# Whole 16 KB ring slots for the experts in the dense part's memory, and rooms of their own for inputs and router tables

## The chip, the cores and the metric

The kernel runs on one core of a Trainium2 chip. A core has five engines with an instruction queue each: TensorE (PE, with weight loads listed as PEld), VectorE (DVE), ScalarE (ACT), GpSimd (POOL) and SyncE (SP), and 16 DMA engines, which the queues of SP, ACT and POOL feed here. On-chip memory (SBUF) has 128 partitions; a tile "128x4096" of float32 takes 16 KB in each of them, 2 MB in all. The metric is the device time of one execution in microseconds (us).

## The reference

256 tokens of 1024 features go through three blocks and a mixture of experts:

```
x = first_block(x, ...)    # twice: ffn, convolution or attention, ffn
x = second_block(x, ...)   # latent attention and block attention, gated; ffn with a convolution
h = rms_norm_3(x, norm_mix_w); proj = h @ w_in                  # third block
merged = sigmoid(gate_a) * (att @ w_branch_attn) + sigmoid(gate_s) * (ssd @ w_branch_ssd)
x = x + merged @ w_out
h2 = rms_norm_3(x, norm_ffn_w)
x = x + hierarchical_moe(h2, ...)    # 64 experts in 8 groups; 2 of the best group's 8 for each token
return rms_norm_3(x, final_norm_w)
...
def expert_block(args):
    xblk, e = args
    hid = silu(xblk @ w_gate[e]) * (xblk @ w_up[e])     # 1024 -> 512
    return hid @ w_down[e]                              # 512 -> 1024
```

All is float32. An expert's three matrices are 6.29 MB.

## The kernel before

**Dense part** (to about 1940 us). x lies as 8 chunks of 128 features by 256 tokens. Each weight matrix comes in pieces of up to 1 MB through SP's queue (L428) into three buffers `raw`; ACT rounds a piece to its high part `wh` (L444), DVE takes the rest as the low part `wl` (L445), and PE multiplies both with the high and low halves of the input. These halves are made by `split` (ACT L620 for the high, DVE L621 for the low half) out of x, or of another stage's result, and lie in units of `up`, a pool of 24 tiles of 4 KB in each partition that hands its tiles round: inputs of the stages, results between stages, attention's operands, rope tables and later the router's constants `rconst` and weights `wr` all take units `u` of it. The order on each engine is not written out: a scheduler sets it when the kernel is built, from the dependences and the pools' rooms.

**Foreseeing** (`foresee`, L1507 on). Near the end of the third block two experts are guessed from the first chunks of x, and fetched before the routing is known. Each needs three slots of 16 KB; a slot is four `up` units, and each unit has a transfer of its own of 512 KB (L1565).

**Experts** (`moe`). The routing orders the experts by their tokens; 42 have some here, and one of them a second block of tokens. The ring holds nine slots, three experts: slots 0 to 5 are the 24 `up` units that `foresee` filled, slots 6, 7 and 8 are whole tiles `ring` in pools of their own (8 lies where `xk` was and comes last). `load(j)` (L1807) reads the expert's number into a register and issues its slots on SP's queue, 4 transfers for a slot of units, 1 for a whole tile (L1816); it is called two experts ahead, and each transfer waits until the block that read the slot's former content is through. Transfers carry `cond=n1 > j`: for an expert without tokens the instruction is stepped over without moving data. So two of three experts come as 12 transfers of 512 KB, the third as 3 of 2 MB. `block` multiplies 64 tokens with gate and up (L1894, L1896), applies silu and product (L1900, L1901), and multiplies with down (L1914, L1916); the weighted result goes into the sums `po` during the next block (L1884). The order is written out by hand in this part. Beyond the last expert with tokens all engines branch out (L1936).

**End.** SP fetches the final gain `fin` into the first unit of slot 0 (L1943), ACT sums the squares of `po` (L1948), DVE multiplies `po` with the gain (L1950), and then computes the factor of the norm (L1951 and the lines of `newton2`); both scale, and the result goes out.

Of the kernel before, what the change touches and what calls it, by code (L numbers as in the profile page):

```python
# [11 lines left out]
F = mybir.dt.float32  # L12
# [13 lines left out]
# experts by place: two that are loaded ahead, then the others, the one with the most tokens at place BIG, whose next  # L26
# ones follow it; those of the 8th most and on come first. RANK: the place in the order of the numbers of tokens
BIG = 7
RANK = [0, 1] + list(range(9, 7 + BIG)) + list(range(2, 9)) + list(range(7 + BIG, NEXP))
# blocks of up to 64 tokens of an expert: the first of each expert, then what the first two and the largest of the  # L30
# others can have more, as at most 7, 3, 2 experts have over 64, 128, 192 of the 512 places
# [6 lines left out]
UNITS = 24  # L38
# [6 lines left out]
# products whose sums have PSUM banks of their own rather than half a bank  # L45
# [11 lines left out]
# steps of the last product before the router's first sums: more than the 16 of its first two chunks  # L57
# [7 lines left out]
def _lin_pieces(kc, sizes, kp):  # L65
    """(first chunk, end, first k, end) of each piece; chunks of several pieces go in pairs"""
    pieces, c = [], 0
    if kp < kc:
        for c in range(0, len(sizes), 2):
            for k in range(0, kc, kp):  # L70
                pieces += [(c, c + 1, k, k + kp), (c + 1, c + 2, k, k + kp)]
        return pieces
    for n in sizes:
        pieces.append((c, c + n, 0, kc))
        c += n
    return pieces
# [134 lines left out]
def _const(cc, cz, a, b):  # L211
    """constants a to b: those from negl to ident in cz, exact in float32r, the others in cc"""
    o, e = CC["negl"][0], CC["inv3"][0]
    return cc[:, a:b] if b <= o else cc[:, a - e + o:b - e + o] if a >= e else cz[:, a - o:b - o]
# [122 lines left out]
def weave(n, first, second, fill, per, lag=1):  # L337
    """first(i) and, lag rounds later, second(i); then per steps of fill, and what second(i) returns, if anything"""
# [11 lines left out]
def newton(nc, v, y, t):  # L350
    """y = v ** -0.5"""
# [10 lines left out]
def newton2(nc, v, y, t):  # L362
    """y = v ** -0.5 for two columns, whose steps alternate; t: [P, 4]"""
# [16 lines left out]
class Main:  # L380
# [19 lines left out]
    def chunks(self, n):  # L400
        """n chunks [P, T]"""
# [3 lines left out]
    def tokens(self):  # L405
        """two token tiles [P, D]"""
# [24 lines left out]
    def load_split(self, dram, off, blocks, width=P):  # L431
        """one piece of weights, as a function from its block number to the high and low parts"""
# [21 lines left out]
    def linear(self, name, xk, epi, c_from=0, c_to=None, wide=0, one=True, among=None):  # L454
        """a generator, one step per piece of weights (the first wide of them as one, by k);
        xk(k): [P, 2T] float32r, high halves then low halves;
        epi gets the chunks that a piece completes, [(chunk, PSUM)], the products with the low halves in columns of
        their own unless one is set; a step of among follows each k of each chunk"""
# [33 lines left out]
        def bank(c):  # L492
            """the place of chunk c: half a bank if it has one sum"""
# [74 lines left out]
    def evac(self, pss, outs, rb=None):  # L568
        """outs = the sums, times rb"""
# [6 lines left out]
    def evac2(self, pss, outs, rb):  # L576
        """outs = the sums of the halves times rb"""
# [6 lines left out]
    def resid2(self, scale):  # L584
        """x += scale times the sums of the halves"""
# [26 lines left out]
    def split(self, src, dst, scale=None):  # L612
        """dst[:, :T] = high half of src * scale, dst[:, T:] = the rest, exactly"""
# [10 lines left out]
    def split_units(self, n):  # L624
        us = [self.tl(self.up, [P, 2, 2 * T], "u", R32) for _ in range((n + 1) // 2)]
        return lambda k: us[k // 2][:, k % 2]

    def colsum(self, srcs, square=True, scale=None, per=1):
        """[P, T] in PSUM: over all features, the same in every partition"""
# [25 lines left out]
    def colsum2(self, srcs, out, scale=None, per=4, first=True):  # L655
        """out: [P, 2] in PSUM, sums of squares over all features by token; the first use of its bank or not"""
# [13 lines left out]
    def spread(self, rc, r):  # L670
        """r: two columns of tokens as a row in every partition"""
# [5 lines left out]
    def scaled(self, gname, cols=None):  # L677
        """x * g, split, and the rstd that is still to be applied, computed once the next weights are under way"""
        dst = self.split_units(8)
# [29 lines left out]
    def renormed(self, g1, g2):  # L709
        """for x = rms_norm(x) * g1, to be set by calling the last result, what scaled(g2) would give of it. With  # L710
        S = sum x^2 and S1 = sum (x g1)^2 the product of both rstds is (S1 / D + eps (S / D + eps)) ** -0.5"""
# [3 lines left out]
        dst = self.split_units(8)  # L715
# [24 lines left out]
    def normed(self, r, g):  # L740
        """x * r * g, split"""
        nc = self.nc
        dst = self.split_units(8)
# [6 lines left out]
    def row(self, a):  # L750
        """two columns of tokens as a row in every partition of PSUM"""
# [33 lines left out]
    def conv_module(self):  # L785
# [6 lines left out]
        # the shift m of the layer norm: the mean of the first seven chunks  # L792
# [27 lines left out]
        def epi(items):  # L820
# [8 lines left out]
            if j == 1:  # L829
                # not ahead of the work of the parts before  # L830
# [8 lines left out]
        # d = y - m, of which only the last chunk has a sum  # L839
# [33 lines left out]
    def stick(self):  # L873
# [18 lines left out]
        def pair(j):  # L892
            """logits of two heads and their softplus"""
# [40 lines left out]
    def rope(self, xs, tabs, half, ys):  # L934
        """ys = rotated xs; every 2 * half rows of a chunk are a head, and tabs its cosines and sines (the first half
        of those negative)"""
# [12 lines left out]
    def softmax(self, parts, scale, neg=None):  # L949
        """parts: (qT, kT) pairs contracted and summed, times scale or, by q, minus neg; returns exp(s - max)  # L950
        [P, (q0k0 | q1k0 | q1k1)] and its sums"""
# [53 lines left out]
    def second_attn(self):  # L1005
# [4 lines left out]
        xk, r, _, finish = self.renormed("fg1", "an2")  # L1010
# [30 lines left out]
        # the rstd of q goes into the softmax  # L1041
# [46 lines left out]
    def gates(self, name, xk, dst, bias, c0, r=None):  # L1088
        """tanh(z / 2), from which sigmoid(z) = (1 + tanh(z / 2)) / 2"""
# [12 lines left out]
    def gated(self, name, y, g):  # L1102
        """g = (1 + g) * (y @ w)"""
# [8 lines left out]
    def merge(self, ga, wb, yb, gb, wo, among=None):  # L1112
        nc = self.nc
        ms = self.split_units(8)
# [79 lines left out]
    def third_mix(self):  # L1194
# [29 lines left out]
        # step sizes and lam: x @ w as [high; low] of w times (high | low) of x, whose four parts are summed  # L1224
# [45 lines left out]
        # running sums of da within each half of the tokens, by head and token (twice, as high and low parts), and  # L1270
        # by token and head: nb = the sums at the token k of a block, minus them, minus them plus what is between
# [20 lines left out]
        # differential attention  # L1292
# [36 lines left out]
        # convolved inputs of the other branch  # L1329
# [69 lines left out]
        def half(i):  # L1399
            """the decays times C.B of two heads, for blocks of tokens (k, q): (1, 1), (0, 0), (0, 1)"""  # L1400
# [12 lines left out]
            for hh in range(2):  # L1413
# [5 lines left out]
                # above the diagonal, where cb is 0, any finite exponential will do  # L1419
# [65 lines left out]
    def route_consts(self):  # L1485
        nc = self.nc
        self.rcn = self.tl(self.up, [P, D], "u")
        nc.scalar.dma_start(self.rcn[:, :sum(n for _, n in RC.values())], self.ap["rconst"])
        self.wrb = self.tl(self.up, [P, D], "u")
# [7 lines left out]
    def logits(self, k):  # L1497
        """adds the part of chunk k to the router's sums"""
# [8 lines left out]
    def foresee(self):  # L1507
        """a generator: guesses from the first two chunks of x the two experts with the most tokens and loads them.
        They come first in route(), whether they have any tokens or not"""
# [41 lines left out]
        # what puts them first: more tokens than any other can have  # L1551
# [5 lines left out]
        self.ring = []  # L1557
        for j in range(2):
            e = nc.values_load(it[0:1, j:j + 1], engines=[ET.SP], min_val=0, max_val=NEXP - 1,
                               skip_runtime_bounds_check_because="the expert of a one-hot column")  # L1560
            for i in range(3):
                us = [self.tl(self.up, [P, D], "u") for _ in range(4)]
                for q, u in enumerate(us):
# [415 lines left out]
```

## Time and profile before

| what | us |
|---|---|
| median of 3 runs (lowest to highest) | 2597.13 (2595.78 to 2599.96) |
| profiled execution: span from first to last instruction | 2596.5 |
| what lies around the span | 0.6 |
| PE busy | 2477.3 (95%) |
| DVE busy | 1578.1 (61%) |
| ACT busy | 1266.9 (49%) |
| DMA queue of SP: share of 16 engines | 60.1% |
| SP's transfers of quarters, waited for by its queue | 131.8 |

The slices of the page divide the span in 40 equal parts of 65 us; a digit is the busy share in tenths. The granted clock of PE is 0.985 of full speed over the span. Window rows give, for each stretch, the busy time and the count of instructions of each engine, then the granted clock, the mean busy share of the DMA engines (a little over 1 when they are full), and the rate in GB/s. Timeline rows give start, duration, engine (a q behind it for its queue: branches, DMA issues), line, operation, output and input tile, count, and in brackets the idle time before it with what ended it. A row with "x24" stands for 24 instructions from the first's start to the last's end.

### The profile page before, as it was taken

What the parts mean: (1) busy time and instruction counts of PE and PEld (TensorE: products, weight loads), DVE (VectorE), ACT (ScalarE), POOL (GpSimd) and SP (SyncE); (2) the same over time, 40 slices, a digit from 0 to 9 for tenths busy, and PEclk for the clock granted to TensorE, in tenths of its full rate; (3) what the DMA queues carried; (4) which work ended last, traced back from release to release, by engine and by line L of the source; (5) the groups of instructions that cost most, each with busy time, mean ns of one, the idle gap of its engine ahead of it and who ended that gap; (6) DMA issues with size and microseconds to landing.
All of it is one profiled execution on the core that took longest, in us unless ns stands there. A gap on an engine that the chain in (4) does not pass through costs nothing. (4 is left out here: it accounts for less than half of the span.)

```text
span 2596.5 us, 41179 instructions
## 1 busy us (share of the span) xinstructions
PE 2477.3 (95%) x15468; PEld 1919.1 (74%) x15468; DVE 1578.1 (61%) x3128; ACT 1266.9 (49%) x2402; POOL 29.1 (1%) x62
## 2 busy tenths in 40 slices
PE   8999999999999999999999999999978989999885
PEld 7889888888888888989999889988972333333221
DVE  7768887687654876876799688987751111111111
ACT  6546665565555555765566587966531101111101
POOL 0000000000000000000000000000000000000000
PEclk9999899999999999999999999999989999999998
DMA  6554055555542556434554654434478999999995
GB/s 236 178 190 146 33 179 179 179 196 178 200 156 98 179 174 207 168 131 152 182 184 163 200 181 145 165 115 140 168 288 341 398 378 414 412 417 413 418 413 228
DMA packets 103901, 579.18 MB, mean 223 GB/s; under 512 B 12033, under 2 KB 13057, under 8 KB 68353
## 3 DMA queue, kind: packets, MB, share of 16 engines
q1 hardware_dynamic: 101520, 573.49, 60.1%
q8 instruction: 132, 2.16, 0.3%
q10 hardware_dynamic: 2016, 2.13, 0.3%
q14 instruction: 89, 0.72, 0.1%
q0 software_dynamic: 144, 0.67, 0.1%
HBM read 587.78 MB, written 1.05 MB: 227 GB/s over the span
## 5 line engine op out<-in xcount | busy, mean ns | idle before, releaser
L444 ACT ACTIVATE wh<-raw 128x1024 fp32r<-128x1024 f32 (+1 forms) x636 | 628.1, 991 | 542.1 <-PE pl L489 258.7
L445 DVE TENSOR_TENSOR wl<-raw,wh 128x1024 fp32r<-128x1024 f32 (+1 forms) x636 | 720.8, 1136 | 219.0 <-ACT wh L444 216.2
L489 PE MATMUL pl<-u,wh 128*128 128x512 f32 x2288 | 809.6, 396 | 9.5 <-ACT wh L444 9.5
L490 PE MATMUL pl<-u,wl 128*128 128x256 f32 x2288 | 646.0, 282 | 0.0
L485 PE MATMUL pl<-u,wh 128*128 128x256 f32 x2180 | 616.0, 283 | 3.0 <-ACT u L617 1.9
L487 PE MATMUL pl<-u,wl 128*128 128x256 f32 x2180 | 612.3, 281 | 3.7 <-DVE wl L445 3.7
L486 PE MATMUL pl<-u,wh 128*128 128x256 f32 x2180 | 613.5, 282 | 0.3
L489 PEld LDWEIGHTS pl<-u,wh 128*128 128x128 f32 x2288 | 431.3, 188 | 113.2 <-ACT wh L444 10.0
L490 PEld LDWEIGHTS pl<-u,wl 128*128 128x128 f32 x2288 | 430.5, 188 | 0.3
L485 PEld LDWEIGHTS pl<-u,wh 128*128 128x128 f32 x2180 | 410.9, 189 | 7.0 <-ACT u L617 2.2
L487 PEld LDWEIGHTS pl<-u,wl 128*128 128x128 f32 x2180 | 410.6, 188 | 6.8 <-DVE wl L445 4.6
L486 PEld LDWEIGHTS pl<-u,wh 128*128 128x128 f32 x2180 | 411.4, 189 | 2.9 <-DVE u L621 0.9
L1901 DVE TENSOR_TENSOR h<-s,pgu 64x512 f32<-64x512 f32 x43 | 29.7, 692 | 491.1 <-ACT s L1900 491.1
L1894 PE MATMUL pgu<-u,xe 128*64 128x512 f32 x464 | 211.0, 603 | 18.6 <-PEq L1926 6.7
L1896 PE MATMUL pgu<-u,xe 128*64 128x512 f32 x464 | 211.1, 603 | 0.0
L1894 PEld LDWEIGHTS pgu<-u,xe 128*64 128x64 f32 x464 | 62.4, 139 | 156.5 <-issue 130.9
L1900 ACT ACTIVATE s<-pgu 64x512 f32<-64x512 f32 x43 | 25.3, 589 | 308.8 <-PE pgu L1896 308.8
L581 DVE TENSOR_TENSOR t<-pl,t 128x256 f32<-128x256 f32 x176 | 73.6, 420 | 85.9 <-ACT t L580 85.9
L1894 PE MATMUL pgu<-ring,xe 128*64 128x512 f32 x224 | 104.1, 617 | 20.2 <-DMA ring<-wexp 16.1
L1918 ACT COPY yy<-py 128x512 f32<-128x512 f32 x43 | 25.2, 585 | 177.8 <-PE py L1916 140.9
L1884 PE MATMUL po<-yy,cw 64*128 64x512 f32 x344 | 106.6, 635 | 3.3 <-ACTq L1936 3.3
L1914 PE MATMUL py<-u,hT 128*64 128x512 f32 x232 | 105.8, 598 | 0.5 <-ACT hT L1912 0.5
(450 smaller groups left out, 2852.0 us busy)
## 6 DMA issues: line engine op xcount, KB each, us to landing
u<-wexp SPq DMA_DIRECT2D x360, 512.0 KB
raw<-w_ffi SPq DMA_DIRECT2D x88, 1024.0 KB
ring<-wexp SPq DMA_DIRECT2D x42, 2048.0 KB
raw<-w_ffo SPq DMA_DIRECT2D x64, 704.0 KB
raw<-w_up SPq DMA_DIRECT2D x22, 1024.0 KB
raw<-w_in3x SPq DMA_DIRECT2D x16, 1024.0 KB
raw<-w_pw SPq DMA_DIRECT2D x12, 1024.0 KB
raw<-w_v SPq DMA_DIRECT2D x12, 1024.0 KB
```

The source lines that it names most:

```text
L444: nc.scalar.activation(wh[:, :n], src, AF.Copy)
L445: nc.vector.tensor_tensor(out=wl[:, :n], in0=src, in1=wh[:, :n].bitcast(F), op=OP.subtract)
L485: nc.tensor.matmul(ps[c], lhsT=wh, rhs=x[:, :T], start=st, stop=False, skip_group_check=True)
L486: nc.tensor.matmul(ps[c], lhsT=wh, rhs=x[:, T:2 * T], start=False, stop=False, skip_group_check=True)
L487: nc.tensor.matmul(ps[c], lhsT=wl, rhs=x[:, :T], start=False, stop=k == kc - 1, skip_group_check=True)
L489: nc.tensor.matmul(ps[c], lhsT=wh, rhs=x, start=k == 0, stop=False)
L490: nc.tensor.matmul(ps[c][:, :T], lhsT=wl, rhs=x[:, :T], start=False, stop=k == kc - 1)
L581: self.each(lambda o, t, p: nc.vector.tensor_tensor(out=o, in0=p[:, :T], in1=t, op=OP.add), outs, ts, pss)
L1884: nc.tensor.matmul(po[t_ * 2 + dh], lhsT=cw[64 * dh:64 * dh + 64, t_ * P:(t_ + 1) * P], rhs=yy[64 * dh:64 * dh + 64, :], start=False, stop ...
L1894: nc.tensor.matmul(pgu[0:64], lhsT=xj[:, k], rhs=w(k * D), start=k == 0, stop=k == 7)
L1896: nc.tensor.matmul(pgu[64:128], lhsT=xj[:, k], rhs=w(k * D + 512), start=k == 0, stop=k == 7)
L1914: nc.tensor.matmul(py[0:64], lhsT=hT[:, k], rhs=w(8 * D + k * D), start=k == 0, stop=k == 3)
```

## The change

The pool `up` has 20 units for 24. Four tiles of the same size in a pool `mx` hold the inputs of the stages that are made by `scaled`, `renormed` (for the second attention) and `normed`, and the merged branches in `merge`. The router's constants and weights get a tile `rcw` that exists from the start. In `foresee` the pool `up` is closed, and a pool `rg` is opened in its place with five whole slots: three for the first guessed expert and two for the second. Its third slot, `ring5`, lies in a pool `own` that `moe` opens, and `load(1, (2,))` fetches it there. All nine slots are whole tiles with one transfer of 2 MB each, and the tiles of the end (`fr`, `junk`, `y`) are quarters of slot 0. The room that generated DMA descriptors take on the chip is set to 8192. The rest of the diff takes out comments and docstrings.

```
-UNITS = 24
+UNITS = 20
...
-    def split_units(self, n):
-        us = [self.tl(self.up, [P, 2, 2 * T], "u", R32) for _ in range((n + 1) // 2)]
+    def split_units(self, n, own=False):
+        us = [self.tl(self.mx if own else self.up, [P, 2, 2 * T], "u", R32) for _ in range((n + 1) // 2)]
...
     def scaled(self, gname, cols=None):
-        dst = self.split_units(8)
+        dst = self.split_units(8, True)
...
     def merge(self, ga, wb, yb, gb, wo, among=None):
-        ms = self.split_units(8)
+        ms = self.split_units(8, True)
...
     def route_consts(self):
         nc = self.nc
-        self.rcn = self.tl(self.up, [P, D], "u")
-        nc.scalar.dma_start(self.rcn[:, :sum(n for _, n in RC.values())], self.ap["rconst"])
-        self.wrb = self.tl(self.up, [P, D], "u")
+        n = sum(n for _, n in RC.values())
+        self.rcn, self.wrb = self.rcw[:, :n], self.rcw[:, n:n + 648]
+        nc.scalar.dma_start(self.rcn, self.ap["rconst"])
...
         self.ring = []
+        self.upx.close()
+        rg = self.top.enter_context(self.tc.tile_pool(name="rg", bufs=1, side="right"))
         for j in range(2):
...
-            for i in range(3):
-                us = [self.tl(self.up, [P, D], "u") for _ in range(4)]
-                for q, u in enumerate(us):
-                    o = i * 4096 + q * D
-                    nc.sync.dma_start(u, self.ap["wexp"][ds(e, 1), :, o:o + D].rearrange("o p l -> p (o l)"))
-                self.ring.append(us)
+            for i in range(3 - j):
+                slot = rg.tile([P, 4096], F, name=f"ring{3 * j + i}")
+                nc.sync.dma_start(slot, self.ap["wexp"][ds(e, 1), :, i * 4096:i * 4096 + 4096].rearrange("o p l -> p (o l)"))
+                self.ring.append(slot)
...
         rts = top.enter_context(tc.tile_pool(name="rt", bufs=1))
-        up = top.enter_context(tc.tile_pool(name="up", bufs=UNITS, side="right"))
+        rcw = rts.tile([P, sum(n for _, n in RC.values()) + 648], F, name="rcw")
+        upx = ExitStack()
+        up = upx.enter_context(tc.tile_pool(name="up", bufs=UNITS, side="right"))
         with ExitStack() as ctx:
             m = Main(tc, ap, ctx)
+            m.mx = ctx.enter_context(tc.tile_pool(name="mx", bufs=4))
...
+        big = [ctx.enter_context(tc.tile_pool(name="own", bufs=1)).tile([P, 4096], F, name="ring5")]
...
-        def load(j):
+        def load(j, only=range(3)):
...
-            for i in range(3):
-                slot = ring[(3 * j + i) % NSLOT]
-                w = D if slot[0][0] is not slot[1][0] else 4096
-                for o in range(0, 4096, w):
-                    nc.sync.dma_start(slot[o // D][0][:, :w],
-                                      wx[ds(e, 1), :, i * 4096 + o:i * 4096 + o + w].rearrange("o p l -> p (o l)"),
-                                      cond=n1 > j)
+            for i in only:
+                nc.sync.dma_start(ring[(3 * j + i) % NSLOT],
+                                  wx[ds(e, 1), :, i * 4096:i * 4096 + 4096].rearrange("o p l -> p (o l)"),
+                                  cond=n1 > j)
...
         more = (n2, n3, n4)
+        load(1, (2,))
...
-        fr, junk, *y = (u for u, _ in ring[0])
+        fr, junk, *y = (ring[0][:, q * D:q * D + D] for q in range(4))
...
-    nc = _bacc.Bacc("TRN2", target_bir_lowering=False, num_devices=1)
+    nc = _bacc.Bacc("TRN2", target_bir_lowering=False, num_devices=1, dynamic_dma_scratch_size=8192)
```

The order changes in three places. First DVE's queue at the program's start, before and then after (`rcw` holds the router's constants, `cn` is a small tile of the routing, `u` are the halves of x, `wl` and `raw` the first weights):

```order
L1975 UNCONDITIONAL_BRANCH
L621 SCALAR_TENSOR_TENSOR u_90<-x,pc,u_90 128x256 x2
L621 SCALAR_TENSOR_TENSOR u_91<-x,pc,u_91 128x256 x2
L445 TENSOR_TENSOR wl_123<-raw_76,wh_122 128x1024
L445 TENSOR_TENSOR wl_127<-raw_76,wh_126 128x1024
```

```order
L1978 UNCONDITIONAL_BRANCH
L1638 COPY cn<-rcw 64x1
L621 SCALAR_TENSOR_TENSOR u_94<-x,pc,u_94 128x256 x2
L621 SCALAR_TENSOR_TENSOR u_95<-x,pc,u_95 128x256 x2
L445 TENSOR_TENSOR wl_127<-raw_80,wh_126 128x1024
L445 TENSOR_TENSOR wl_131<-raw_80,wh_130 128x1024
```

The copy out of the router's constants has moved from the routing to the head of DVE's queue; the transfer that it reads, `rcw<-rconst`, is the fifth entry of ACT's queue now, behind four small ones.

Then ACT's queue at the end of `out2`, the second block's output product, and the start of `up2` behind it (`u<-x,pc` are the high halves of `up2`'s input, `t<-x` squares of x), before and after:

```order
L444 ACTIVATE wh_13607<-raw_13605 128x1024
L620 ACTIVATE u_13566<-x,pc 128x256
L662 ACTIVATE t_13627<-x 128x256
L444 ACTIVATE wh_13611<-raw_13605 128x1024
L620 ACTIVATE u_13566<-x,pc 128x256
L662 ACTIVATE t_13630<-x 128x256
L444 ACTIVATE wh_13729<-raw_13727 128x1024
L620 ACTIVATE u_13567<-x,pc 128x256
```

```order
L444 ACTIVATE wh_13615<-raw_13609 128x1024
L663 ACTIVATE t_13634<-x 128x256
L444 ACTIVATE wh_13733<-raw_13731 128x1024
L620 ACTIVATE u_13568<-x,pc 128x256 x2
L620 ACTIVATE u_13569<-x,pc 128x256 x2
L620 ACTIVATE u_13570<-x,pc 128x256 x2
L620 ACTIVATE u_13571<-x,pc 128x256
```

The splits stood one behind each weights' split; now they stand together behind the last but one.

Last SP's queue at the end of the program, where the loads of experts 42 and 43 and the branches stand ahead of the final gain, before (its last six of 24 loads) and after (all six):

```order
L1816 DMA u_21028<-wexp 128x1024
L1816 ISA
L1816 DMA u_21029<-wexp 128x1024
L1816 ISA
L1816 DMA u_21030<-wexp 128x1024
L1936 COMPARE_AND_BRANCH x2
L1936 UNCONDITIONAL_BRANCH x51
L1943 DMA u_21011<-fin 128x1024
```

```order
L1820 DMA ring_21017<-wexp 128x4096
L1820 ISA
L1820 DMA ring_21019<-wexp 128x4096
L1820 ISA
L1820 DMA ring_21021<-wexp 128x4096
L1939 COMPARE_AND_BRANCH x2
L1939 UNCONDITIONAL_BRANCH x51
L1946 DMA ring_21017<-fin 128x1024
```

A slot's four instructions have become one, here as in every load of slots 0 to 5.

## Rows read from the trace of the kernel before

**Rows 1.** The page: PE and the DMA rate in 40 slices of the span.

```profile
PE   8999999999999999999999999999978989999885
...
GB/s 236 178 190 146 33 179 179 179 196 178 200 156 98 179 174 207 168 131 152 182 184 163 200 181 145 165 115 140 168 288 341 398 378 414 412 417 413 418 413 228
```

**Rows 2.** Windows of the expert part: busy us (instructions), clock, DMA share, GB/s.

```profile
1990.00:2010.00 20.00, 19.19 (x92) 6.16 (x90) 4.17 (x8) 2.50 (x5) 1.23 (x2) 1.00 1.01 408
...
2070.00:2090.00 20.00, 16.35 (x70) 5.73 (x68) 2.09 (x4) 1.54 (x3) 0.61 (x1) 0.91 0.86 312
...
2450.00:2550.00 100.00, 88.09 (x389) 26.45 (x385) 13.23 (x26) 9.87 (x19) 4.31 (x7) 0.98 1.02 415
```

**Rows 3.** Windows in which whole slots (three rows), then quarters, flow alone.

```profile
2144.00:2150.00 6.00, 5.17 (x26) 1.96 (x24) 0.00 (x0) 0.58 (x1) 0.00 (x0) 1.00 1.01 419
...
2280.00:2286.00 6.00, 6.00 (x32) 1.87 (x26) 0.00 (x0) 0.27 (x1) 0.00 (x0) 1.00 1.02 434
...
2371.00:2377.00 6.00, 4.42 (x22) 1.55 (x20) 0.00 (x0) 0.58 (x1) 0.00 (x0) 1.00 1.00 426
...
2207.00:2225.00 18.00, 17.19 (x84) 5.55 (x82) 4.17 (x8) 2.32 (x5) 1.09 (x2) 1.00 1.03 408
2252.00:2270.00 18.00, 17.59 (x86) 5.78 (x84) 2.08 (x4) 2.13 (x4) 0.61 (x1) 1.00 1.03 411
```

**Rows 4.** Timeline of SP's queue from 2146 us: first issue's start, time to the last.

```profile
2146.55 29.81 SPq L1816 DMA_DIRECT2D u<-wexp  x24
...
2502.15 40.61 SPq L1816 DMA_DIRECT2D u<-wexp  x24
...
2547.53 28.30 SPq L1816 DMA_DIRECT2D u<-wexp  x24
2581.80 0.36 SPq L1943 DMA_DIRECT2D u<-fin  x1
```

**Rows 5.** Timelines of PE, then ACT, then DVE from 2558 us to the end.

```profile
2558.28 1.09 PE L1894 MATMUL pgu<-ring,xe 128*64 128x512 f32 x1 [3.32 <-DMA ring<-wexp]
...
2572.75 0.59 PE L1916 MATMUL py<-ring,hT 128*64 128x512 f32 x1
...
2579.14 0.60 ACT L1948 ACTIVATE u<-po 128x512 f32<-128x512 f32 x1 [5.10 <-SPq L1936]
...
2581.79 0.19 ACT L1948 ACTIVATION_READ_ACCUMULATOR u<-po 128x1 f32 x1
...
2585.62 2.48 DVE L1950 TENSOR_TENSOR u<-po,u 128x512 f32<-128x512 f32 x4 [14.88 <-DMA u<-fin]
2588.02 0.15 DVE L1951 TENSOR_TENSOR fv<-sq 128x2 f32<-128x2 f32 x1
```

**Rows 6.** Timelines of ACT's queue, DVE and PE at the start; a window there.

```profile
2.15 0.95 ACTq L1197 DMA_DIRECT2D al<-rows  x1
...
6.87 1.68 DVE L621 SCALAR_TENSOR_TENSOR u<-x,pc,u 128x256 fp32r<-128x256 f32 x4 [6.87 <-ACT u L620]
9.32 2.36 DVE L445 TENSOR_TENSOR wl<-raw,wh 128x1024 fp32r<-128x1024 f32 x2 [0.77 <-ACT wh L444]
...
9.34 0.79 PE L489 MATMUL pl<-u,wh 128*128 128x512 f32 x1 [9.34 <-ACT wh L444]
...
12.00:14.00 2.00, 2.00 (x7) 1.70 (x7) 2.00 (x7) 2.00 (x8) 0.00 (x0) 1.00 1.00 417
```

**Rows 7.** The page's transfer of `cz` (KB, us to landing); `rconst` near the dense part's end.

```profile
cz<-consts POOLq DMA_DIRECT2D x1, 656.0 KB, 8.6
...
1810.66 0.33 ACTq L1488 DMA_DIRECT2D u<-rconst  x1
...
1815.19 0.14 DVE L1636 COPY cn<-u 64x1 f32<-64x1 f32 x1
```

**Rows 8.** ACT's timeline at the end of `out2`, and a window there.

```profile
1299.32 0.49 ACT L620 ACTIVATE u<-x,pc 128x256 fp32r<-128x256 f32 x1
...
1270.00:1310.00 40.00, 39.95 (x335) 39.32 (x334) 32.44 (x71) 23.55 (x38) 0.00 (x0) 1.00 0.53 180
```

More of the change, by code (lines that the diff above doesn't have):

```diff
@@ L707, in unhook2, with renormed @@
             hook()
-    def renormed(self, g1, g2):
+    def renormed(self, g1, g2, own=False):
         nc = self.nc
@@ L714, in renormed @@
         nc.vector.tensor_tensor(out=g, in0=self.col(g1, 0, 8), in1=self.col(g2, 0, 8), op=OP.mult)
-        dst = self.split_units(8)
+        dst = self.split_units(8, own)
         for k in range(8):
@@ L742, in normed @@
         nc = self.nc
-        dst = self.split_units(8)
+        dst = self.split_units(8, True)
         for k in range(8):
@@ L1009, in second_attn @@
             nc.scalar.dma_start(rt[a], self.ap["rope2"][:, a * T:(a + 1) * T])
-        xk, r, _, finish = self.renormed("fg1", "an2")
+        xk, r, _, finish = self.renormed("fg1", "an2", True)
         rc = self.rc
@@ L1726, in build @@
         rts = top.enter_context(tc.tile_pool(name="rt", bufs=1))
-        up = top.enter_context(tc.tile_pool(name="up", bufs=UNITS, side="right"))
+        rcw = rts.tile([P, sum(n for _, n in RC.values()) + 648], F, name="rcw")
+        upx = ExitStack()
+        up = upx.enter_context(tc.tile_pool(name="up", bufs=UNITS, side="right"))
         with ExitStack() as ctx:
             m = Main(tc, ap, ctx)
+            m.mx = ctx.enter_context(tc.tile_pool(name="mx", bufs=4))
+            m.rcw = rcw
             m.x, m.cc, m.cz = x, cc, cz
@@ L1744, in build @@
             tc.keep_in_program_order(nc.gpsimd.dma_start(cz.bitcast(R32), ap["consts"][:, o:e]))
-            m.up = up
+            m.up, m.upx, m.top = up, upx, top
             m.sp = ctx.enter_context(tc.tile_pool(name="sp", bufs=2))
@@ L1793, in moe @@
         first = ctx.enter_context(tc.tile_pool(name="first", bufs=1))
-        big = [first.tile([P, 4096], F, name=f"ring{j}") for j in range(6, NSLOT - 1)]
+        big += [first.tile([P, 4096], F, name=f"ring{j}") for j in range(6, NSLOT - 1)]
         sb = ctx.enter_context(tc.tile_pool(name="moe", bufs=1))
@@ L1801, in cst @@
             return _const(cc, cz, o + a, o + (n if b is None else b))
-        ring = [[(u, 0) for u in us] for us in ring] + [[(b, q * D) for q in range(4)] for b in big]
+        ring = ring + big
         wx = ap["wexp"]
-        def load(j):
+        def load(j, only=range(3)):
             if j >= NEXP:
@@ L1860, in moe @@
         last = ctx.enter_context(tc.tile_pool(name="last", bufs=1))
-        big = last.tile([P, 4096], F, name=f"ring{NSLOT - 1}")
-        ring.append([(big, q * D) for q in range(4)])
+        ring.append(last.tile([P, 4096], F, name=f"ring{NSLOT - 1}"))
         def window(b, dst):
@@ L1889, in w @@
             def w(o):
-                u, a = ring[(3 * j + o // 4096) % NSLOT][o % 4096 // D]
-                return u[:, a + o % D:a + o % D + 512]
+                return ring[(3 * j + o // 4096) % NSLOT][:, o % 4096:o % 4096 + 512]
             for k in range(8):
```

## The prediction

> **What bounds the kernel now.** I read the page first (engine shares and the 40 slices), then windows of the expert stage, SP's issue queue, and the timelines of the first 13 and the last 40 us. The page shows two programs one after the other [rows 1]: up to about 1940 us PE is busy in nearly every slice while the DMA engines move about 180 GB/s; behind it the slices stand at 412 to 418 GB/s. The reader is to see that PE sets the end of the dense part, and the transfers that of the expert part. The windows say it more sharply [rows 2]: from 2450 to 2550 PE is busy 88% and the DMA share is 1.02. In 2070 to 2090 that share is only 0.86: there the ring was full, PE was the later one, and the transfers waited for it. So nothing that transfers gain or lose before about 2110 reaches the end; what they do behind it does, through the last block, whose first matmul waited 3.32 us for its slot [rows 5].
>
> **The stream.** In SP's queue [rows 4] groups of three whole slots (2 MB each) alternate with 24 quarters (0.5 MB each). The group of 24 at 2146.55 is the first behind the full ring, that at 2502.15 the last with data (the 24 at 2547.53 are for experts with no tokens and move nothing). Between and with these two lie nine groups, 9 x 24 = 216 quarters, 113.2 MB. The change turns them into 54 whole slots. What that is worth is read off the stretches in which one kind flows alone [rows 3]. Six stretches of whole slots gave 419, 425, 433, 434, 423 and 426 GB/s, mean 426.7; five of quarters 409, 408, 411, 409 and 409, mean 409.2. So 113.2 MB takes 265.4 us for 276.7: **-11.3 us**. With the slowest whole and the fastest quarter stretch (419, 411) it is -5.3, with 434 and 408 it is -16.6. PE doesn't take the bound back: an expert of 6.29 MB takes 14.7 us at 426.7 GB/s. PE's last block runs from 2558.28 to 2573.3, 15.0 us, in which its first four pairs of matmuls ran 1.09 us each for 0.59 [rows 5], about 1.7 us in all; without that a block takes some 13.3 us, less than a transfer either way.
>
> The Trainium skill (DMA: Bandwidth & Descriptors, Where 436 GB/s comes from) says that for transfers between HBM and SBUF the HBM side binds at about 358 GB/s; by that the size of a transfer would change nothing here. The trace disagrees on the figure: both kinds run above 400. That the memory, and not the transfer's shape, sets the rate is nevertheless a rival below.
>
> **The tail.** The last down matmul ends at 2573.3, and the end comes 23 us later. SP is still stepping through the 24 skipped quarters (from 2547.53 for 28.30 us), takes 6.0 us of branches, and only then issues the final gain at 2581.80 [rows 4]. DVE has waited 14.88 us for it when it starts at 2585.62, and the chain L1951 starts at 2588.02 [rows 5]. With the change 6 skipped slots stand in place of 24 quarters; they wait only for the block before the last, so SP is through some 2 us behind the last block's start, and even with its 6.0 us of branches ready before 2573.3. The gain, 3.8 us from issue to its use, is then there by about 2577.5. What is late next are ACT's squares: their last read-out starts at 2581.79 and takes 0.19, so L1951 starts at about 2582.0 for 2588.02: **-6.0 us**. ACT's own delay, 5.10 us in front of the first square, is put down to SP's branch in that row; ACT passes the same branches itself, so I leave it where it is. If SP did hold it, up to 2 us more go; if the issue still comes late, nothing: 0 to -8.
>
> **The start.** `rconst` (128 rows of 1009 floats, 516 KB) moves from the dense part's end to the fifth place on ACT's queue at the very start, and the copy `cn<-rcw` that reads it becomes DVE's first instruction, ahead of the first splits of x. Queued behind that wait are all splits L621, all low halves of weights L445, and PE, whose products need both. Before, DVE began at 6.87 [rows 6], with 0.77 us idle in front of its first L445. ACT's fourth issue starts at 2.15 and takes 0.95, so rconst is issued at about 3.1. No row has this transfer beside the first loads. Bounds: on a quiet core it was issued at 1810.66 and its copy ran at 1815.19, under 4.5 us [rows 7], which would land it at 7.6 and cost nothing over the 0.77. The constants `cz`, 656 KB beside weight loads on another queue, took 8.6 us; counted from 3.1 that gives 11.7, counted from about 8, when x and the first weights are through, 16 and more, a cost of 8. I take 8.6 from the issue, since that row is the nearest in size, place and company: landing 11.7, copy 0.14, first split at 11.85, so 4.98 later, less the 0.77: **+4.2 us** (0 to +8). From 12 on PE and DVE are both busy all of the time [rows 6], so the loss isn't caught up.
>
> By the Trainium skill (DMA: Bandwidth & Descriptors, Queues, rings and completion order) an engine takes turns between the queues that it has work for, packet by packet; by that rconst would get about half of the rate and land within its lower bound. The constants' row disagrees: 656 KB in 8.6 us is 76 GB/s, a fifth of the stream. It is the first rival.
>
> **The dense part.** The split inputs get four units of their own, so each stage's input waits for the last reader of the one before. Of all stages that shows in one place: at the end of `out2` ACT's splits of x for `up2` now stand in a bunch behind the last weights' split, where before one stood between each two. Before, the last split ran at 1299.32, and PE was busy 39.95 of 40 us there [rows 8]. Eight splits at 0.49 are 3.9 us on ACT, of which PE needs the first only; the others lie beside its products, two chunks by k. I take **+0.5** (0 to +3). Fewer `up` units (20 for 24) wait for nothing else: on the other engines the order and the waits read the same. The reopening itself is hidden: expert 0 and two thirds of expert 1 are fetched into five slots from about 1900 on, the sixth a little later, and block 0 starts at 1953, after routing. I count it at nothing; if it were late, the full ring at 2070 would absorb it.
>
> **The sum** against the execution that the profile shows: 4.2 + 0.5 - 11.3 - 6.0 = -12.6. Its span was 2596.5, with 0.6 us around it, which is the median of the runs, 2597.1. So the span comes to 2583.9 and the time to **2584.5 us**.
>
> **Rivals.**
> - *The start is hidden* (rconst lands by 7.6): +0.5 - 11.3 - 6.0 = -16.8, 2580.3. For it the quiet transfer's 4.5 us; against it the constants' 8.6, and DMA engines that are full at that time, so that 516 KB has to displace something. 0.15.
> - *Whole slots are no faster as a stream*: the 6 us stretches are short, and what they gained may be given back where the kinds change over; with the memory as the bound all whole is as fast as the mixture. Then 4.2 + 0.5 - 6.0 = -1.3, 2595.8. Against it: all six stretches lie above all five others. 0.13.
> - *The tail stays* (the gain is issued late all the same, or the squares move with it): 4.2 + 0.5 - 11.3 = -6.6, 2590.5. For it: the profile blames a branch of SP for ACT's wait; against: the skipped issues fill SP up to the branches. 0.13.
> - *Slower: large transfers run below the mixture.* A slot can be refilled only when all of it is read, and counts as landed only when its slowest part is in; with fewer, larger pieces in the queue the engines may fall dry between them. The stage has shown such a rate: 408 GB/s in 1990 to 2010, at a DMA share of 1.01 [rows 2]. From 2110 to 2558 at 414 GB/s 185.5 MB move; at 400 GB/s they take 463.7 us for 448, +15.7, in all +14.4, 2611.5. It decides from 408 GB/s down, where it costs 6.5 and the total passes +5.2. Against it the same six stretches. 0.06.
> - The forecast keeps 0.53.
>
> **Numbers.** A difference of 0.2%, 5.2 us, is what a measurement can tell here. Beyond it on the fast side lie nearly all of the forecast, the first rival and a bit more than half of the third: 0.75. Within it the second rival, the rest of the third and a little of the forecast: 0.17. Beyond it on the slow side the fourth and the worst ends of the start together with the second: 0.08. All ends added give 2574 and 2602; the range with 8 in 10 is 2575 to 2597, from near the best case over the third and second rival.
>
> **What will show it.** DVE's first split at about 11.9 and PE's first product 3 to 5 us behind 9.34: the start. Windows of 100 us behind 2150 at 425 GB/s or more, and last block's first matmul some 7 us earlier than 2558.28 (4.7 later by start and boundary, 11.3 earlier by the stream): the stream. The final gain issued by the time of the last down matmul, and L1951 8.8 us behind it for 14.7: the tail. Windows at 414 would overthrow the stream's term, a first split before 8 the start's, and L1951 still waiting for the gain the tail's.

## The result, and the profile after

The changed kernel took 2577.06 us in the median of 4 runs (2575.2 to 2581.64), the kernel before 2597.86 beside it: a ratio of 0.9919, 95% interval 0.9906 to 0.9932. Run again in five rounds it took 2579.97 (2578.24 to 2582.1), ratio 0.9927 (0.9913 to 0.994). It is faster by 19 to 21 us, where 12.6 were forecast. The time lies inside the range, on its fast side.

The profiled execution of the changed kernel has a span of 2579.9 us and took 2581.64; the later profiles show 1.7 to 2.0 us around their spans, so the first profile of the kernel before stands for about 2598.2, not 2596.5 + 0.6 as the sum took it. The stream of the changed kernel, as windows (columns as in [rows 2]):

```profile
2150.00:2250.00 100.00, 96.35 (x450) 32.03 (x446) 14.60 (x28) 10.83 (x21) 4.32 (x7) 1.00 1.01 427
2250.00:2350.00 100.00, 96.76 (x454) 31.67 (x454) 16.68 (x32) 11.99 (x24) 4.94 (x8) 1.00 1.01 427
2350.00:2450.00 100.00, 94.09 (x436) 30.32 (x432) 14.59 (x28) 11.23 (x22) 4.32 (x7) 1.00 1.01 427
2450.00:2550.00 100.00, 89.31 (x410) 28.72 (x412) 14.59 (x28) 10.84 (x21) 4.32 (x7) 1.00 1.01 427
```

427 GB/s stands where [rows 2] have 415, in each window. To time the stream, take ACT's silu of block 11, the first behind the full ring, and of the last block: first the kernel before, then the changed one (timelines of ACT).

```profile
2123.95 0.59 ACT L1900 ACTIVATE s<-pgu 64x512 f32<-64x512 f32 x1 [7.40 <-PE pgu L1896]
...
2567.02 0.59 ACT L1900 ACTIVATE s<-pgu 64x512 f32<-64x512 f32 x1 [11.38 <-PE pgu L1896]
```

```profile
2127.64 0.59 ACT L1903 ACTIVATE s<-pgu 64x512 f32<-64x512 f32 x1 [7.32 <-PE pgu L1899]
...
2557.65 0.59 ACT L1903 ACTIVATE s<-pgu 64x512 f32<-64x512 f32 x1 [7.77 <-PE pgu L1899]
```

443.1 us before, 430.0 now: the stream gives 13.1. Up to 1.6 of that is PE's clock: in the kernel before PE waits 3.32 us for the last block's first slot [rows 5], and from 2558.0 to 2561.5 its granted clock is 0.51, so that four pairs of matmuls take 3.3 us, not 1.7. The changed kernel's last block starts 9.3 us sooner, without that wait and at full clock (timeline of PE):

```profile
2549.03 0.59 PE L1897 MATMUL pgu<-ring,xe 128*64 128x512 f32 x1
```

The tail, in the order of [rows 5] (timelines of PE, ACT, DVE, and SP's queue):

```profile
2563.39 0.59 PE L1919 MATMUL py<-ring,hT 128*64 128x512 f32 x1
2566.84 2.78 PE L1888 MATMUL po<-yy,cw 64*128 64x512 f32 x8 [2.86 <-ACTq L1939]
...
2568.26 0.60 ACT L1951 ACTIVATE ring<-po 128x512 f32<-128x512 f32 x1 [3.59 <-PE po L1888]
...
2568.98 2.85 DVE L1953 TENSOR_TENSOR ring<-po,ring 128x512 f32<-128x512 f32 x4 [7.61 <-ACT ring L1951]
2571.75 0.15 DVE L1954 TENSOR_TENSOR fv<-sq 128x2 f32<-128x2 f32 x1
...
2564.32 0.36 SPq L1946 DMA_DIRECT2D ring<-fin  x1
```

The final gain is issued 0.3 us behind the last down matmul (which ends at 2564.0), no longer 8.5. DVE's chain L1954 starts 7.8 us behind that matmul, before 14.7: 6.9 won. ACT's first square waits for PE now, 4.3 us behind the last down matmul; in [rows 5] it waited for SP, 5.8 behind. What the chain comes behind is DVE's own product with the gain (L1953); ACT's last square is done 0.7 us before it. The start, as in [rows 6]:

```profile
3.00 0.73 ACTq L1490 DMA_DIRECT2D rcw<-rconst  x1
...
13.08 0.14 DVE L1638 COPY cn<-rcw 64x1 f32<-64x1 f32 x1 [13.08 <-DMA rcw<-rconst]
13.21 1.67 DVE L621 SCALAR_TENSOR_TENSOR u<-x,pc,u 128x256 fp32r<-128x256 f32 x4
...
13.84 1.19 PE L489 MATMUL pl<-u,wh 128*128 128x512 f32 x2 [13.84 <-DVE u L621]
```

DVE starts 6.3 us later and PE's first product comes 4.5 later; matched matmul for matmul, PE runs 4.8 us behind the kernel before from 60 to 300 us. The trace's DMA packets show what the landing at 13.1 is made of. The 128 packets of `rconst` (4036 bytes each) run from 8.3 to 12.6 us, though it was issued at 3.0: until then ACT's queue moves packets of 512 and 256 bytes for the small transfers ahead. So it waited 5.3 us and moved for 4.3; on the quiet core, before, it moved for 2.4. That the small transfers caused the wait is read from this order; no run puts `rconst` ahead of them. So far 4.8 - 13.1 - 6.9 = -15.2. The rest is in the dense part, which the forecast had at +0.5: block 0 starts at 1952.7 for 1953.2, so the 4.8 lost at the start are won back on the way. A stretch of the first block's attention shows how. A round of two heads ends with a group of ten small products; the kernel before, then the changed one (timelines of PE):

```profile
785.51 1.54 PE L890 MATMUL pa<-a,cz 128*128 128x128 f32 x10
...
796.40 1.54 PE L890 MATMUL pa<-a,cz 128*128 128x128 f32 x10
```

```profile
781.38 1.54 PE L891 MATMUL pa<-a,cz 128*128 128x128 f32 x10
...
792.08 1.54 PE L891 MATMUL pa<-a,cz 128*128 128x128 f32 x10
```

10.89 us before, 10.70 now. PE waits for nothing in either, at a granted clock of 1.00; the linear products between (L485 to L487) follow each other at 0.113 to 0.114 us for 0.117 to 0.118.

### The profile page after: what moved, and what is told of

It reads as the page before. It is cut to its first block, busy times and chain, and to the rows that moved or that the text cites. A ratio compares the mean times of both kernels' runs of the same rounds, so it can differ in the third digit from the quotient of the medians.

```text
span 2579.9 us, 40094 instructions
## 1 busy us (share of the span) xinstructions
PE 2470.7 (96%) x15468; PEld 1910.6 (74%) x15468; DVE 1578.1 (61%) x3128; ACT 1267.1 (49%) x2402; POOL 29.2 (1%) x62
## 5 line engine op out<-in xcount | busy, mean ns | idle before, releaser
L485 PE MATMUL pl<-u,wh 128*128 128x256 f32 x2180 | 614.7, 283 | 3.3 <-ACT u L617 1.9
L487 PE MATMUL pl<-u,wl 128*128 128x256 f32 x2180 | 611.0, 281 | 4.1 <-DVE wl L445 4.1
L487 PEld LDWEIGHTS pl<-u,wl 128*128 128x128 f32 x2180 | 412.6, 189 | 7.4 <-DVE wl L445 5.1
L485 PEld LDWEIGHTS pl<-u,wh 128*128 128x128 f32 x2180 | 410.4, 189 | 7.4 <-ACT u L617 2.2
L1897 PE MATMUL pgu<-ring,xe 128*64 128x512 f32 x688 | 312.2, 605 | 29.9 <-DMA ring<-wexp 18.4
L1899 PE MATMUL pgu<-ring,xe 128*64 128x512 f32 x688 | 312.5, 605 | 0.0
L1897 PEld LDWEIGHTS pgu<-ring,xe 128*64 128x64 f32 x688 | 93.5, 139 | 233.7 <-issue 211.5
L1917 PE MATMUL py<-ring,hT 128*64 128x512 f32 x344 | 159.5, 607 | 0.5 <-ACT hT L1915 0.5
L1919 PE MATMUL py<-ring,hT 128*64 128x512 f32 x344 | 159.5, 607 | 0.0
L1917 PEld LDWEIGHTS py<-ring,hT 128*64 128x64 f32 x344 | 44.2, 138 | 108.2 <-issue 75.7
```

The lines of the kernel that those rows point to most:

```text
L485: nc.tensor.matmul(ps[c], lhsT=wh, rhs=x[:, :T], start=st, stop=False, skip_group_check=True)
L487: nc.tensor.matmul(ps[c], lhsT=wl, rhs=x[:, :T], start=False, stop=k == kc - 1, skip_group_check=True)
L1897: nc.tensor.matmul(pgu[0:64], lhsT=xj[:, k], rhs=w(k * D), start=k == 0, stop=k == 7)
L1899: nc.tensor.matmul(pgu[64:128], lhsT=xj[:, k], rhs=w(k * D + 512), start=k == 0, stop=k == 7)
L1917: nc.tensor.matmul(py[0:64], lhsT=hT[:, k], rhs=w(8 * D + k * D), start=k == 0, stop=k == 3)
L1919: nc.tensor.matmul(py[64:128], lhsT=hT[:, k], rhs=w(8 * D + k * D + 512), start=k == 0, stop=k == 3)
```

## The experiments

**The changed kernel again** (no edit).

> The changed kernel once more, for a second profile and an interval. My account: the start costs 4.9 us (DVE's first split at 13.2, PE's first product at 13.8), the stream runs at 427 GB/s from 2120 on, the final gain is on chip before the squares are done; the median stays at 2577, and the 5 us by which the profiled execution was slower than the three others is scatter of PE's clock in the dense part and in the first blocks. Rival: the profiled execution is the typical one, then the median comes to 2581.

Median 2579.97; the profiled execution had a span of 2576.5. So the rival is nearer on the median, but the executions scatter by 4 us around it. In this second profile the start, the stream (silu to silu 430.2) and the tail (7.5 us) are nearly as in the first; what differs most is PE's pace in `up2` (below). Between these two profiles the three terms agree within 0.3 us; the total doesn't.

**The copy late.** The router's transfer stays at the start, its copy goes behind the one ahead of it in the routing:

```
-        V.tensor_copy(cn[:, 0:1], pc[0:64, 0:1])
+        first = V.tensor_copy(cn[:, 0:1], pc[0:64, 0:1])
...
-        V.tensor_copy(cn[:, 3:4], rk("pmod", p=64))
+        with self.tc.issue_after(first.ins):
+            V.tensor_copy(cn[:, 3:4], rk("pmod", p=64))
```

> Only the copy out of the router's constants is put back behind the copy before it in the routing; the transfer stays at the program's start. Theory (DVE's wait for that transfer delays all by 4.9 us and nothing catches up): first split at 6.9, first product at 9.3, end 4.9 us sooner, about 2572 for 2577. Rival A (the early transfer itself takes its 1.3 us of full DMA engines from x and the first weights): 1 to 2 us less gain, 2573.5. Rival B (the dense part absorbs the late start somewhere): no gain, 2577.

2571.9 us (2571.61 to 2572.36), ratio 0.9894 (0.9879 to 0.9909). Timelines of DVE and PE:

```profile
6.96 1.68 DVE L621 SCALAR_TENSOR_TENSOR u<-x,pc,u 128x256 fp32r<-128x256 f32 x4 [6.96 <-ACT u L620]
...
9.13 0.79 PE L489 MATMUL pl<-u,wh 128*128 128x512 f32 x1 [9.13 <-ACT wh L444]
```

One instruction moved, and PE runs level with the kernel before (0.1 us ahead at 100 us). The theory's 4.9 is shown by the profile; the medians differ by 8.1, and the start doesn't explain the other 3. Rivals A and B fall: the transfer itself costs nothing at the start, and the dense part doesn't absorb the wait. This version beats both kernels, by 26.8 us against the one before.

**The transfers late too.** As far back as the scan's last square:

```
+            self.late = nc.scalar.activation(sq, xx, AF.Square)
...
+        with self.tc.issue_after(self.late.ins):
+            nc.scalar.dma_start(self.rcn, self.ap["rconst"])
...
```

> The router's three transfers are put behind the last square of the scan on ACT's queue, near where they stood before the change; the copy follows them. Theory: as with the copy alone, 2572, and at most 1.3 us better than it, since 516 KB at about 400 GB/s no longer stand among the first loads. Rival: the late transfers and copy stand in the way of the routing, as they did before, and cost 1 us or more against the copy alone.

2577.27 (2571.12 to 2580.65). Its profile (span 2569.4) has the same start as the copy alone and an end 0.8 us sooner; the runs scatter by 9.5 us. The median is 5.4 us above the copy alone's, as the rival has it, but the ratios' intervals overlap (0.9901 to 0.9929 and 0.9879 to 0.9909). Nothing is shown between the two, and the copy alone was the steadier one.

**The skipped quarters back, alone.**

```
+                w = D if j >= 42 and slot < 6 else 4096
+                for o in range(0, 4096, w):
```

> The loads for experts from 42 on, which are all stepped over, go to slots 0 to 5 in quarters again: 24 skipped issues at the end for 6, nothing else moves. Theory (the skipped issues held the final gain, and that the end): last matmul unchanged, final gain issued some 8 us behind it, end 7 us later, 2584. Rival (the tail is short for another reason, such as ACT's branches or the whole tile at the end): unchanged, 2577.

2588.39 (2587.38 to 2589.67), 8.4 more than the changed kernel beside it. Timelines of PE, ACT and DVE, and SP's queue:

```profile
2561.86 0.59 PE L1922 MATMUL py<-ring,hT 128*64 128x512 f32 x1
...
2569.30 0.60 ACT L1954 ACTIVATE ring<-po 128x512 f32<-128x512 f32 x1 [6.16 <-SPq L1942]
...
2575.99 2.48 DVE L1956 TENSOR_TENSOR ring<-po,ring 128x512 f32<-128x512 f32 x4 [16.13 <-DMA ring<-fin]
2578.39 0.15 DVE L1957 TENSOR_TENSOR fv<-sq 128x2 f32<-128x2 f32 x1
...
2571.94 0.35 SPq L1949 DMA_DIRECT2D ring<-fin  x1
```

The gain comes 9.5 us behind the last matmul, DVE waits 16.13 us for it, and the chain starts 15.9 behind that matmul, where the kernel before had 14.7 and the changed one 7.8. The skipped issues are shown to be the cause of the long tail, and ACT's first square is back to waiting for SP. In SP's queue they follow each other at 0.46 us, which for 18 more of them is 8.3 us.

**What sets the stream's rate.** Three kernels change only how slots 0 to 5 are filled for experts 2 to 41 (and in the third, where the matmuls find each quarter): four transfers of a quarter (1), two of a half (3), and two of a half whose 8 KB in a partition go to two places (4):

```
1:  w = D if 1 < j < 42 and slot < 6 else 4096
3:  w = 2 * D if 1 < j < 42 and slot < 6 else 4096
4:  dst = ring[slot].rearrange("p (a b l) -> p b a l", a=2, b=2)
    for b in range(2):
        nc.sync.dma_start(dst[:, b], src[:, :, b * 2 * D:(b + 1) * 2 * D]...)
```

> The changed kernel with slots 0 to 5 filled by four transfers of 512 KB (4 KB in each partition) again, for experts 2 to 41; the tiles stay whole, foreseen and skipped loads too. Theory (the transfer's shape sets the stream's rate): 409 GB/s where quarters flow, 414 over 100 us, last block 11 to 13 us later, 2589 for 2577. Rival (the stream gained because slots come free or are asked for sooner, not by shape): windows stay at 427, 2577.

> Slots 0 to 5 by two transfers of 1 MB, 8 KB in each partition. Theory of a fixed cost for each piece in a partition: with 409.2 GB/s for 4 KB and 426.7 for 16 KB the time per byte falls as 1/length, which gives 420.7 for 8 KB alone and a third of the loss, some 4 us, 2581. Rival (a threshold between 4 and 8 KB, or the number in flight): 427 GB/s and 2577.

> Two transfers of 1 MB for each of slots 0 to 5, as in the run with halves, but each puts its 8 KB of a partition down as two pieces of 4 KB that don't lie next to each other (the order of the quarters in the slot is changed, and the matmuls read them so). Theory (the length of the piece sets the rate): as with quarters, 414 GB/s over 100 us, about 442 us from block 11 to block 42, some 2592. Rival (the number and size of the transfers): as with halves, 422 GB/s, 432 us, 2585.

One window of each, in this order:

```profile
2250.00:2350.00 100.00, 97.17 (x454) 31.74 (x452) 14.59 (x28) 11.42 (x22) 4.30 (x7) 1.00 1.02 414
```

```profile
2250.00:2350.00 100.00, 97.17 (x453) 31.79 (x454) 15.50 (x30) 11.42 (x22) 4.30 (x7) 1.00 1.01 422
```

```profile
2250.00:2350.00 100.00, 97.17 (x454) 31.51 (x450) 14.78 (x29) 11.43 (x22) 4.92 (x8) 1.00 1.02 414
```

| filled by | transfers a slot | piece | GB/s | silu to silu, us | median, us |
|---|---|---|---|---|---|
| whole slots | 1 | 16 KB | 427 | 430.0, 430.2 | 2577.06, 2579.97 |
| halves | 2 | 8 KB | 422 | 433.7 | 2585.36 |
| halves in two pieces | 2 | 4 KB | 414 | 442.6 | 2591.28 |
| quarters | 4 | 4 KB | 414 | 444.5 | 2592.66 |

The rate goes with the length of the piece that lies together in a partition, not with the number or size of the transfers: the last two rows differ by a factor of two in number and agree in rate, the two rows of halves agree in number and differ by 8 GB/s. (Of the 1.9 us between the last two rows, up to 1.5 is again the half clock in the last block, which the run with quarters has and the one with two pieces hasn't.) Halves lose 3.6 us of the 14.4 that quarters lose, a bit less than the third that a fixed cost for each piece gives.

The traces' DMA packets show that cost itself. A packet is one piece of one partition. From 2150 to 2450 us one of 4 KB takes its engine 163 ns in the mean (164 in the run with two pieces), one of 8 KB 315, one of 16 KB 618. Four small ones so take 34 ns more than one of 16 KB, two halves 12 more: some 11 to 12 ns for each packet, whatever its length.

The Trainium skill (DMA: Bandwidth & Descriptors, Why small descriptors are slow) names such a cost, some 3 cycles for each packet, where 32 bytes take one; at 4 KB against 16 KB that is an estimate of under 2%, while the stretches of one kind in [rows 3] differ by 4%, so the direction agrees and the size doesn't.

**Quarters by partitions.** The same number of transfers with 16 KB pieces, each to 32 of the 128 partitions:

```
+                n = 32 if 1 < j < 42 and slot < 6 else P
+                for o in range(0, P, n):
+                    nc.sync.dma_start(ring[slot][o:o + n], wx[ds(e, 1), o:o + n, ...])
```

> The same four transfers of 512 KB for each of slots 0 to 5, but each of 32 partitions with the whole 16 KB of a partition. Theory (the length of the piece in a partition decides): 427 GB/s, 2577 as with whole slots. Rival (the number of transfers, their fixed cost and SP's waits for earlier ones decide): 414 GB/s, 2589, as the quarters.

3015.13 us, ratio 1.1574 (1.1547 to 1.1601): neither theory. Two windows:

```profile
2150.00:2250.00 100.00, 74.49 (x298) 24.49 (x294) 10.43 (x20) 7.74 (x15) 3.07 (x5) 0.90 1.01 281
...
2350.00:2450.00 100.00, 61.67 (x216) 19.86 (x216) 6.60 (x13) 5.24 (x10) 2.46 (x4) 0.81 1.01 231
```

The engines count as busy (1.01) at 281 and 231 GB/s; a packet of 16 KB takes 1049 ns here in the mean, for 618. A transfer to a quarter of the partitions is slow for a reason of its own, which no run here separates, so this run says nothing on the length of the piece; the run with two pieces took its place.

**PE's pace in the dense part.** Two more profiles of the kernel before came first.

> The kernel before, for a second profile. Of the five profiles with whole tiles all show the second block's up2 (1305 to 1425 us) passed 2 to 6 us sooner against the first profile of the kernel before, with PE busy throughout. Theory (PE's pace in a stage differs between executions of one program): this profile shows a gain of that kind against the first one too, or a loss elsewhere. Rival (the change made the stage shorter): the second profile agrees with the first there within 0.5 us.

> As the run before it, a third profile of the kernel before: with two more of them it is to be seen whether the pace in up2 scatters or is the same each time.

2595.07 and 2605.5 us. In both a round of heads takes 10.89 or 10.90, and `up2` passes within 0.1 us of the first profile: in three profiles the kernel before has one pace. The rival is favoured: the change made these stages shorter. Then all inputs were put back into `up`, with everything else as changed:

```
-UNITS = 20
+UNITS = 24
...
-        us = [self.tl(self.mx if own else self.up, [P, 2, 2 * T], "u", R32) ...]
+        us = [self.tl(self.up, [P, 2, 2 * T], "u", R32) ...]
```

> The changed kernel without the inputs' own room: UNITS 24 again and all split inputs in up; ring slots, router table and tail as changed. In the seven profiles of whole tiles the dense part passes 707 to 811, 1020 to 1310 and 1740 to 1850 us of the first profile's time in 5.0 us less than in the three profiles of the kernel before, each stretch alike in all of them, and up2 (1310 to 1430) in 4.3 less in most. Theory (where the inputs lie, or when they are free, sets PE's pace there): these stretches take as long as in the kernel before, block 0 starts 5 to 9 us later, 2585 to 2588. Rival (the pace hangs on the shift of PE against the other engines by the later start, or on the rest of the memory's layout): the stretches are as short as in the changed kernel, 2579.

2585.74 (2580.27 to 2594.59), 6 us slower than the changed kernel run on its own. Half of that is the start: the router's constants land at 15.0 us in this profile, and PE runs 8.0 us behind the kernel before, not 4.8. Timeline of PE:

```profile
783.57 1.54 PE L891 MATMUL pa<-a,cz 128*128 128x128 f32 x10
...
794.47 1.54 PE L891 MATMUL pa<-a,cz 128*128 128x128 f32 x10
```

10.90 us again, and of 5.0 us that the stretches named in the expectation had gained 3.6 are lost. The exception is `up2`: it keeps its quicker pace here, as in seven of the nine profiles with the changed layout, so that part (4.3 us in those executions, nothing in the other two, of which the first profile is one) isn't due to the inputs' room. Nor is the later start the cause: with the copy late PE is level with the kernel before, and the same stretches are 5.0 us shorter. Last, the inputs keep their room, but it lies behind the weight buffers, which move by 16 KB with it, as does the small tile `pc`; no engine's order changes:

```
-            m.mx = ctx.enter_context(tc.tile_pool(name="mx", bufs=4))
...
             m.wp = ctx.enter_context(tc.tile_pool(name="wp", bufs=4))
+            m.mx = ctx.enter_context(tc.tile_pool(name="mx", bufs=4))
```

> The changed kernel with the inputs' own room behind the weight buffers on chip instead of ahead of them; the order of every engine is the same. In the first block's attention a round of two heads takes 10.70 us on PE in the changed kernel and 10.90 in the kernel before and with inputs in up. Theory (their room being their own, that is when it is free and what else shares it, sets the pace): 10.70, and 2579 in all. Rival (the place on chip sets the pace): another pace, 10.90 or between, and the time of the dense part moves with it.

2585.29 (2584.26 to 2590.01). Timeline of PE:

```profile
779.04 1.54 PE L891 MATMUL pa<-a,cz 128*128 128x128 f32 x10
790.03 1.54 PE L891 MATMUL pa<-a,cz 128*128 128x128 f32 x10
```

10.99 us: slower than either, with the same instructions in the same order. Other stages are quicker for it: from 811 to 1020 us of the first profile's time this run gains 3.1 us on the kernel before, the changed kernel 0.1. So it isn't that the inputs have a room of their own, nor when it is free, but where inputs and weight buffers lie on the chip. Which of them, and by what mechanism, stays open.

## Why the prediction was right, and what it had missed

- **The stream** was right in mechanism and rate: 426.7 GB/s forecast, 427 measured, -11.3 forecast, -13.1 measured. The size was off by the count: the group of 24 quarters at 2102.70 us, issued as the ring filled, was left out of the 216; with its 12.6 MB the same rates give -12.6. Beside the rate, the measured 13.1 holds up to 1.6 of half clock in the last block, which the sum left out. The rival of no gain had a condition, the memory as the bound, that the runs with quarters and with two pieces refute; a rate below the mixture's, as the slower rival has it, appears only with transfers to 32 partitions, which the change doesn't make.
- **The tail** was right: -6.0 forecast, -6.9 measured. The step left open, whether SP holds ACT's squares, came out on the fast side (1.5 us sooner); that DVE's product would end last was not foreseen.
- **The start** was right in place, and near in size in part by luck: +4.2 forecast, +4.8 measured. The landing came at 13.1, not 11.7, and DVE's first split 6.3 us later, not 5.0, but 1.5 of it was absorbed where the sum had 0.77. The constants' row (78 GB/s, not 76) gave a fair total without the reason: half of the time went by before the first packet, not in company on the engines. In the other profiles with the early copy PE is 4.9 to 8.7 us behind. The rival of a hidden start fell, though the total, 2577 to 2580, lies nearer to its 2580.3 than to the forecast.
- **The dense part** is the step that failed. "I take +0.5" priced the inputs' rooms by order and waits alone. Measured are -5.0 in stretches that are nearly alike in every profile (-4.5 to -5.4), and another -4.3 in `up2` in most executions. At the end of `out2` itself the bunch of splits cost nothing: PE passed 1280 to 1300 in 0.3 us less. No row of before could have given this, since no wait and no duration in it points to the place of a tile on the chip; a range of a few us on either side for "moved memory" would have been the honest price.
- **The sum**: 4.8 - 5.0 - 13.1 - 6.9 = -20.2 against medians that differ by 18.7 and 20.8 and first profiles that differ by 16.6. What goes to and fro beside it is larger than the forecast allowed: `up2`, and the blocks 0 to 11, where the granted clock is 0.5 for some of PE's matmuls (block 0 to block 11 takes 163.5, 158.5 and 168.0 us in three profiles of the kernel before, 167.8 in both of the changed one). In the prediction's range, all ends added give 2572.5 and 2602.8, not 2574 and 2602. Without the 5.0 in the dense part, which the forecast didn't have, the time would stand at about 2582, near the forecast; with it, it stands 2 us above the range's fast end.

## What to carry to other kernels

When a stream fills the DMA engines, look at the bytes that one transfer puts down together in each partition: 16 KB pieces in place of 4 KB for two thirds of the bytes raised the rate from 414 to 427 GB/s here, and halving the number of transfers at the same piece left it at 414. An early tile without a dependence lets a scheduler hoist its first reader to the head of an in-order queue: see which instruction stands first after a change of rooms, and what stands ahead of the transfer that it waits for. And price a move of memory with some scatter of its own on either side, even where no order changes.

## What the runs showed of the hardware

- A DMA packet's time is a fixed part and a part by length: 163, 315 and 618 ns for 4, 8 and 16 KB, so some 11 to 12 ns for each packet, and 27 bytes a ns on each engine.
- A stage of PE's float32r products runs at one of several paces with all waits gone: 10.70, 10.90 or 10.99 us for the same round by where inputs and weight buffers lie, at a granted clock of 1.00 in all of them.
- One program's executions can differ in a stage's pace: `up2` at 71 or 73 matmuls in 8 us (windows of the changed kernel's two profiles), again at a granted clock of 1.00; what decides it isn't shown:

```profile
1340.00:1348.00 8.00, 8.00 (x71) 8.00 (x70) 7.95 (x16) 5.76 (x10) 0.00 (x0) 1.00 0.61 193
```

```profile
1340.00:1348.00 8.00, 8.00 (x73) 8.00 (x72) 7.96 (x16) 5.99 (x10) 0.00 (x0) 1.00 0.66 214
```

- With two thirds of the bytes in transfers to 32 partitions at a time, the stream runs at 231 to 281 GB/s while the engines count as busy throughout.
